# A decoder block on one core: the FFN input product without full blocks, with the first two block products of five pairs done ahead

## The chip, the cores and the metric

The kernel runs on one core of a Trainium2 chip. The metric is the time of one execution in microseconds (us) on the device. The engines are PE (TensorE, matrix products into PSUM banks of 128 x 512 float32), DVE (VectorE), ACT (ScalarE), POOL (GpSimd) and SP (SyncE, which issues nearly all transfers here). Each engine works through its own list of instructions in order and waits where one of them needs a result that isn't there yet.

## What is computed

One decoder block on 1024 tokens of width 1024: a dilated attention and a causal convolution module in parallel, merged by gates, projected and added to x; then a SwiGLU FFN with hidden width 2816. Everything is float32. The part that matters here is the end of the mix and the first half of the FFN:

```python
merged = jax.nn.sigmoid(z_ga) * y_attn + jax.nn.sigmoid(z_gc) * y_conv
x = x + rms_norm(merged @ w_mix_out[l], g_post_mix[l])
h = rms_norm(x, g_pre_ffn[l])
gate, up = jnp.split(h @ w_ffn_in, 2, axis=-1)
x = x + rms_norm((jax.nn.silu(gate) * up) @ w_ffn_out, g_post_ffn[l])
```

## The kernel before

**Products.** A float32 product is made of three fast ones: each operand is split into a high part (a cast, on ACT) and a low part (the difference, on DVE or POOL), and PE adds high x high, high x low and low x high. `split` does this for activations (lines 1286 and 1287), `part` (190, 191) and `both` (208, 209) for weights. `unit` multiplies one block of 128 output features by 512 tokens: 8 steps of three matmuls (lines 318 to 320). `prod` does the same over 4 steps (lines 334 to 336).

**Ticks.** After every step of three matmuls `tick` is called. It runs steps that `later` has put at that tick, then, at every `PIECE`-th tick, one piece of weight preparation from the queue `pieces`, then one step of each background generator in `gens`; a generator that yields n rests for n ticks. All of this only sets the order in which instructions are put on each engine's list.

**Weights.** The list `jobs` holds all weight blocks in order of use. `load_ahead` issues their transfers on SP up to a job, `queue_split` puts their pieces into the queue and moves the counter `queued` past them, `flush` runs what is left of a job's pieces. A pair of blocks ("row1", "row2") is a gate block and the up block that belongs to it, and is prepared by `quarters` in six steps: 0 splits A11 and A12, 1 makes the sums s12, 2 splits S1 and S2, 3 makes s34, 4 splits S3 and S4, 5 splits A22. `pair` is called ahead of each pair: it loads, queues and flushes what isn't done yet, and places steps 3 to 5 of this pair and 0 to 2 of the next at later ticks.

**The seven-product pair.** `winograd` computes a pair (2 x 2 blocks: gate and up by two halves of the tokens) with seven products in place of eight: A11 x B11, A12 x B21, S2 x T2, S1 x T1, S3 x T3, S4 x B22, A22 x T4. The B's are quarters of the activations h (two halves of the features by two halves of the tokens), T1 to T4 sums of them, made by `quarter_sums`. The products add up in the banks X, Z and V; f11, f22, f12 and f21 take the results out on DVE and ACT, and `sums` makes the operands of the last product of the FFN and stores them.

**The stretch in question.** The mix product goes over eight tiles of 128 tokens (line 1697). Behind each tile `mix_norm` runs in the background: two squares on ACT (1396), a row factor on DVE (`rstd_rows`, 1383 to 1388), gain and residual (1403, 1407), a store of the rows (1414), the second norm (1418, 1420). At tiles 3 and 7 the four tiles of a half are transposed on PE (1428), taken out with the gain on ACT (1434) and split. Then come the first `PLAIN` = 2 blocks of the FFN in full, as `ffn_half`: for each half of the tokens a gate unit with Silu and an up unit. The first halves of both run while tile 7 is normalised, the second halves while `quarter_sums` makes T1 to T4. The other 20 blocks are pairs through `winograd`.

## Time and profile before

| what | value |
|---|---|
| median of 3 runs | 1690.35 us (1689.8 to 1692.89) |
| the profiled execution | 1690.83 us, of which its span 1689.0 us |
| busy share of the span | PE 99%, DVE 75%, ACT 48%, POOL 30% |
| granted clock of PE | 0.999 |

The span runs from the first to the last instruction in the trace. "L334" is line 334 of the kernel, and a helper's line stands for all who call it. In the rows of groups the first number behind the bar is the busy time of the group in us, the second the mean ns of one; then comes the engine's idle time before them and who ended it. In the rows in order of time the first number is the start in us, the second the duration; an arrow in brackets says how long the engine had waited and for whom. In the rows of waits stand the sum, the number and the longest. "p" is a PSUM bank, "b" a buffer of 128 x 1024, "c" one of 128 x 512, "d" one of a ring of three.

### The profile page before, as it was taken

The page shows a single profiled execution, that of the slowest core. Times are in us where ns is not written, and L with a number is a line of the kernel's source. Part 1 is how long each engine was busy: PE and PEld are TensorE (multiplying, and loading weights), DVE is VectorE, ACT ScalarE, POOL GpSimd, SP SyncE. Part 2 cuts the span into 40 slices and gives each one's busy share as a digit, 9 for nine tenths or more (in the row PEclk, how much of TensorE's full clock was granted, in tenths as well). Part 3 has the DMA queues.
Part 4 walks back from the last instruction along what each step waited for, and adds up shares of the span by engine and source line. Part 5 has one row for each costly group of instructions (what it writes and reads, how often), then busy time and mean ns, then how long its engine had stood idle before and what let it go on. Part 6 is the DMA issues. An engine that isn't in the chain of part 4 may idle for free.

```text
span 1689.0 us, 23464 instructions
## 1 busy us (share of the span) xinstructions
PE 1676.4 (99%) x8167; PEld 1403.7 (83%) x8167; DVE 1259.8 (75%) x2209; ACT 818.9 (48%) x1599; POOL 513.4 (30%) x399
## 2 busy tenths in 40 slices
PE   9999999999999999999999999999999999999998
PEld 7788888888888889999888888888888888888886
DVE  6789988788999777778886855765655566677686
ACT  6344334344444588888713456533333333354453
POOL 0017777888886265765200300000000000000000
PEclk9999999999999999999999999999999999999999
DMA  4252433455566987888998523032233222494334
GB/s 168 104 187 88 150 125 131 137 195 178 183 174 162 282 269 224 241 232 250 300 294 313 200 88 118 26 131 94 94 114 111 94 94 102 170 376 125 111 121 156
DMA packets 162563, 283.36 MB, mean 168 GB/s; under 512 B 47249, under 2 KB 78988, under 8 KB 162444
## 3 DMA queue, kind: packets, MB, share of 16 engines
q1 hardware_dynamic: 161948, 281.42, 51.1%
q8 instruction: 64, 1.05, 0.3%
q14 instruction: 55, 0.45, 0.1%
q0 software_dynamic: 352, 0.18, 0.1%
q10 hardware_dynamic: 144, 0.26, 0.0%
HBM read 191.10 MB, written 95.42 MB: 170 GB/s over the span
## 4 chain that ended last, share of the span: by engine, by line
PE 93%; DMA 3%; DVE 1%; POOL 1%; issue 1%; ACT 1%; SPq 0%; DVEq 0%; ACTq 0%; POOLq 0%
PE p L334 15%; PE p L335 15%; PE p L336 15%; PE p L1968 12%; PE p L966 5%; PE p L1697 5%; PE p L318 5%; PE p L320 5%; PE p L319 5%; PE p L967 3%; PE p L1082 2%; PE p L1153 2%; PE p L578 2%; PE p L1120 2%; DMA b<-dact 1%
## 5 line engine op out<-in xcount | busy, mean ns | idle before, releaser
L334 PE MATMUL p<-b,b 128*128 128x512 f32 x1204 | 468.7, 389 | 0.5 <-ACT c L353 0.3
L335 PE MATMUL p<-b,b 128*128 128x512 f32 x1204 | 468.4, 389 | 0.0
L336 PE MATMUL p<-b,b 128*128 128x512 f32 x1204 | 468.4, 389 | 0.0
L334 PEld LDWEIGHTS p<-b,b 128*128 128x128 f32 x1204 | 226.0, 188 | 48.6 <-DVE c L862 1.0
L336 PEld LDWEIGHTS p<-b,b 128*128 128x128 f32 x1204 | 226.0, 188 | 46.9
L335 PEld LDWEIGHTS p<-b,b 128*128 128x128 f32 x1204 | 226.0, 188 | 46.8
L1968 PE MATMUL p<-b,b 128*128 128x512 f32 x924 | 209.6, 389 | 0.0
L1968 PEld LDWEIGHTS p<-b,b 128*128 128x128 f32 x924 | 173.4, 188 | 36.0
L708 DVE SCALAR_TENSOR_TENSOR p<-b,par,p 128x511 f32<-128x511 f32 (+14 forms) x232 | 163.6, 740 | 0.0
L318 PE MATMUL p<-b,b 128*128 128x512 f32 x368 | 147.0, 399 | 0.0
L966 PE MATMUL p<-b,b 128*128 128x512 f32 x384 | 144.1, 407 | 0.0
L320 PE MATMUL p<-b,b 128*128 128x512 f32 x368 | 143.5, 390 | 0.0
L319 PE MATMUL p<-b,b 128*128 128x512 f32 x368 | 143.5, 390 | 0.0
L208 ACT CAST b<-d 128x1024 fp32r<-128x1024 f32 x86 | 90.6, 1054 | 105.2 <-POOL d L229 55.1
L209 POOL TENSOR_TENSOR b<-d,b 128x1024 fp32r<-128x1024 f32 x44 | 107.0, 2431 | 79.6 <-ACT b L208 72.3
L209 DVE TENSOR_TENSOR b<-d,b 128x1024 fp32r<-128x1024 f32 x42 | 51.3, 1222 | 101.1 <-ACT b L208 101.1
L1287 DVE TENSOR_TENSOR b<-b,b 128x512 fp32r<-128x512 f32 x133 | 92.5, 700 | 22.2 <-ACT b L1286 20.2
L967 PE MATMUL p<-b,b 128*128 128x256 f32 x384 | 107.7, 281 | 0.0
L1286 ACT CAST b<-b 128x512 fp32r<-128x512 f32 x133 | 82.3, 621 | 48.9 <-PE p L1968 18.6
L1095 ACT ACTIVATE c<-c,stat 128x128 f32<-128x128 f32 (+1 forms) x192 | 85.4, 449 | 13.4 <-DVE stat L1085 12.2
L1697 PE MATMUL p<-b,b 128*128 128x512 f32 x384 | 89.4, 391 | 0.0
L208 ACT CAST b<-b 128x1024 fp32r<-128x1024 f32 x47 | 49.6, 1054 | 81.4 <-POOL b L236 37.3
(233 smaller groups left out, 2915.1 us busy)
## 6 DMA issues: line engine op xcount, KB each, us to landing
b<-w_in SPq DMA_DIRECT2D x30, 512.0 KB, 4.9
dk<-c SPq DMA_DIRECT2D x48, 256.0 KB, 4.5
dq<-c SPq DMA_DIRECT2D x48, 256.0 KB, 3.5
b<-dq SPq DMA_DIRECT2D x48, 256.0 KB, 4.6
b<-dk SPq DMA_DIRECT2D x48, 256.0 KB, 6.8
b<-w_fi SPq DMA_DIRECT2D x24, 512.0 KB, 5.3
d<-w_in SPq DMA_DIRECT2D x23, 512.0 KB, 4.0
dqS<-c SPq DMA_DIRECT2D x44, 256.0 KB, 2.2
```

The source lines that it names most:

```text
L209: self.wsplit.tensor_tensor(lo, x, f(hi), op=OP.subtract)
L318: nc.tensor.matmul(ps, hi[:, s], a, start=kt == 0, stop=False)
L319: nc.tensor.matmul(ps, hi[:, s], b, start=False, stop=False)
L320: nc.tensor.matmul(ps, lo[:, s], a, start=False, stop=kt == nk - 1)
L334: nc.tensor.matmul(ps, hi[:, s], a, start=first and kt == 0, stop=False, skip_group_check=True)
L335: nc.tensor.matmul(ps, hi[:, s], b, start=False, stop=False, skip_group_check=True)
L336: nc.tensor.matmul(ps, lo[:, s], a, start=False, stop=kt == 3, skip_group_check=True)
L708: nc.vector.scalar_tensor_tensor(A[i][:, j:], src[i][:, :H - j], w[i], A[i][:, j:], op0=OP.mult, op1=OP.add)
L966: nc.tensor.matmul(ps, a, w, start=kt == 0, stop=kt == KT - 1, skip_group_check=True)
L967: nc.tensor.matmul(ps[:, 256:], b, w[:, :256], start=False, stop=kt == KT - 1, skip_group_check=True)
L1697: nc.tensor.matmul(banks[tt][nh], st, wt[:, nh * H:(nh + 1) * H], start=bool(kt == 0 and a), stop=bool(kt == KT - 1 and b))
L1968: nc.tensor.matmul(acc[t], x, y, start=first and e == 0, stop=last and e == 2, skip_group_check=True)
```

## The change

There is no block in full any more; all 22 are pairs. For the first `HEAD` = 5 pairs the two products that need only the first half of the tokens (A11 x B11 and A12 x B21) are done right behind the mix product by `head`, with the A11 and A12 weights loaded and split as jobs of their own, and their banks X kept. Then `tail` does the other five products of each of these pairs. The gate and row blocks of these pairs are loaded again for the sums, and step 0 of `quarters` does nothing for them. The last four tiles of tokens are no longer transposed together behind tile 7: `last_tokens` transposes each tile by itself some ticks after its norm, takes it out half on ACT and half on DVE, and makes its part of the sums; behind tile 7 it splits T2, T1, T3, B22 and T4 in this order. `tail` calls `need`, which issues what of these splits hasn't been issued. PSUM is one set of eight banks in this stretch. `limit` keeps the head weights from being loaded before tile 7.

```diff
-PLAIN = 2
+HEAD = 5
...
+    limit = 1 << 30
+    headed = ()
+
     def load_ahead(self, i):
+        i = min(i, self.limit)
...
         if c == 0:
+            if i in self.headed:
+                return
             h, w = self.both(r1)
             o["A11"], o["A12"] = (h[:, l], w[:, l]), (h[:, r], w[:, r])
...
-        while self.queued < min(self.sent, i + 1):
+        while self.queued < min(self.sent, min(i, self.limit) + 1):
...
-        todo = [(1, lambda: self.quarters(i, 3)), (8, lambda: self.quarters(i, 4)), (10, lambda: self.quarters(i, 5))]
+        short = i in self.headed
+        a, b = (4, 8) if short else (8, 10)
+        todo = [(1, lambda: self.quarters(i, 3)), (a, lambda: self.quarters(i, 4)), (b, lambda: self.quarters(i, 5))]
         if n < len(J) and J[n][2] == "row1":
             todo += [(LD, lambda: self.load_ahead(n + 1))]
-            todo += [(k, lambda c=c: self.quarters(n + 1, c)) for c, k in enumerate(PC)]
+            pc = PC if not short else (10, 10, 14) if n + 1 in self.headed else (10, 12, 18)
+            todo += [(k, lambda c=c: self.quarters(n + 1, c)) for c, k in enumerate(pc)]
             if self.conv_sums:
                 todo.append((22, self.channel_sum))
             self.queued = n + 2
...
+    def head(self, w, T, f11):
+
+        nc = self.nc
+        hi, lo = w
+        X, x1 = self.bank(), self.half()
+        self.prod(X, (hi[:, :H], lo[:, :H]), T["B11"], True, False)
+        nc.scalar.copy(x1, X)
+        Z = self.bank()
+        self.prod(Z, (hi[:, H:], lo[:, H:]), T["B21"], True, True)
+        return X, f11(Z, x1)
...
+    def tail(self, W, T, X, need, f12, f21, f22):
+
+        nc = self.nc
+        x2, v1 = self.half(), self.half()
+        need("T2")
+        self.prod(X, W["S2"], T["T2"], False, False)
+        nc.scalar.copy(x2, X)
+        V = self.bank()
+        need("T1")
+        self.prod(V, W["S1"], T["T1"], True, False)
+        nc.scalar.copy(v1, V)
+        need("T3")
+        self.prod(X, W["S3"], T["T3"], False, False)
+        f22(X, v1)
+        v1 = None
+        need("B22")
+        self.prod(V, W["S4"], T["B22"], False, True)
+        rest = f12(V, x2)
+        V = x2 = None
+        need("T4")
+        self.prod(X, W["A22"], T["T4"], False, True)
+        rest()
...
+        if tt > 3:
+            yield from self.last_tokens(tt, hn)
+            return
...
+                y = self.feature(x, kt)
+                nc.scalar.activation(y, ps.rearrange("p (t n) -> p t n", t=4), AF.Copy, scale=self.col(C_PREF + kt))
...
+    def last_tokens(self, tt, hn):
+
+        nc = self.nc
+        o = (tt - 4) * 128
+        if tt == 4:
+            self.raw2 = [self.slot() for _ in range(4)]
+
+        def two(x):
+            return x[:, 2 * o:2 * o + 256]
+
+        add, stt = nc.vector.tensor_tensor, nc.vector.scalar_tensor_tensor
+        yield 6
+        for q in range(2):
+            ps = self.bank()
+            for i in range(4):
+                kt = 4 * q + i
+                nc.tensor.transpose(ps[:, i * 128:(i + 1) * 128], hn[:, kt * 128:(kt + 1) * 128], self.ident)
+            if q == 1:
+                hn = None
+            for i in range(4):
+                kt = 4 * q + i
+                d = two(self.raw2[kt // 2])[:, kt % 2 * 128:kt % 2 * 128 + 128]
+                if i % 2 == 0:
+                    nc.scalar.activation(d, ps[:, i * 128:(i + 1) * 128], AF.Copy, scale=self.col(C_PREF + kt))
+                else:
+                    nc.vector.tensor_scalar(d, ps[:, i * 128:(i + 1) * 128], self.col(C_PREF + kt), None, op0=OP.mult)
+            ps = None
+            yield 0
+        b11, b12, b21, b22 = self.raw1[:2], self.raw2[:2], self.raw1[2:], self.raw2[2:]
+        for i in range(2):
+            add(two(b11[i]), two(b11[i]), two(b12[i]), op=OP.subtract)
+        if tt > 5:
+            t2 = self.t2
+            for i in range(2):
+                stt(two(t2[i]), two(b11[i]), -1.0, two(b22[i]), op0=OP.mult, op1=OP.subtract)
+        if tt < 7:
+            yield 0
+            for i in range(2):
+                add(two(b12[i]), two(b22[i]), two(b12[i]), op=OP.subtract)
+            return
+        T = self.T
+        self.raw1 = self.raw2 = self.g_mix = self.t2 = None
+
+        def keep(name, x):
+            for k in range(4):
+                y = self.split(self.feature(x[k // 2], k), H)
+                T[name].append((y[:, :H], y[:, H:]))
+                if k % 2:
+                    x[k // 2] = None
+                yield (0, 1)[k % 2]
+
+        yield from keep("T2", list(t2))
+        yield from keep("T1", b11)
+        for i in range(2):
+            add(two(b12[i]), two(b22[i]), two(b12[i]), op=OP.subtract)
+        yield 0
+        yield from keep("T3", b12)
+        yield from keep("B22", b22)
+        for i in range(2):
+            stt(b21[i], t2[i], -1.0, b21[i], op0=OP.mult, op1=OP.subtract)
+            t2[i] = None
+            yield 1
+        yield from keep("T4", b21)
...
+    def early_sums(self):
+        b11, b22 = self.raw1[:2], self.raw2[2:]
+        self.t2 = [self.slot() for _ in range(2)]
+        for i in range(2):
+            a, b, c = (x[i][:, :512] for x in (self.t2, b11, b22))
+            self.nc.vector.scalar_tensor_tensor(a, b, -1.0, c, op0=OP.mult, op1=OP.subtract)
+            yield 1
...
+    heads = [job(aps["w_fi"][j]) for j in range(HEAD)]
+    fi = [pair2(j) for j in range(FT)]
+    B.headed = [fi[j] for j in range(HEAD)]
...
-            B.banks(g=6, s=2)
+            B.banks(g=8)
...
+        if tiles[0] == 7:
+            B.limit = 1 << 30
+            for n, j in enumerate(heads):
+                B.later(max(8 * n, 3), lambda j=j: B.load_ahead(j))
+                B.later(max(8 * n, 3) + 8, lambda j=j: B.queue_split(j))
+            B.later(16 + 8 * HEAD - 22, lambda: B.load_ahead(fi[0]))
+            for c, n in ((0, 12), (1, 12), (2, 6)):
+                B.later(16 + 8 * HEAD - n, lambda c=c: B.quarters(fi[0], c))
+            B.later(10, lambda: B.bg(B.early_sums()))
...
-    def ffn_half(j, hf, W):
-        o = B.half()
-        ps = B.unit(W[0], B.rhs(B.h2[hf]), KT)
-        nc.scalar.activation(o, ps, AF.Silu)
-        ps = B.unit(W[1], B.rhs(B.h2[hf]), KT)
-        nc.vector.tensor_tensor(o, ps, o, op=OP.mult)
-        held[j, hf] = o
...
-    for j in range(PLAIN):
-        Ws.append((B.weights(fi[j][0]), B.weights(fi[j][1])))
-        ffn_half(j, 0, Ws[j])
-    B.finish(norms[-1])
-    B.g_mix = None
-    h2 = [[(x[:, :H], x[:, H:]) for x in y] for y in B.h2]
-    qs = B.bg(B.quarter_sums(B.h2f, (h2[0][:4], h2[0][4:], h2[1][4:])))
-    h2 = None
-    for j in range(PLAIN):
-        ffn_half(j, 1, Ws[j])
-        Ws[j] = None
-    B.summed = lambda: None
-    B.first_sums(qs)
...
+    todo, silus = [], []
+    for j in range(HEAD):
+        f11, *rest = outs(j)
+        B.flush(heads[j])
+        X, r = B.head(B.hl.pop(heads[j]), B.T, f11)
+        silus.append(r)
+        if j >= 2:
+            while silus:
+                silus.pop(0)()
+        todo.append((X, rest))
+    X = rest = r = None
+
+    def need(name):
+        while len(B.T[name]) < 4:
+            next(norms[-1][0])
...
+    for j in range(FT):
+        w = B.pair(fi[j])
         if j == FT - 1:
             for k in range(LEAD):
                 loads(k)
             B.bg(first())
-        B.winograd(w, B.T, f11, f12, f21, f22)
+        if j < HEAD:
+            X, rest = todo[j]
+            todo[j] = None
+            B.tail(w, B.T, X, need, *rest)
+            X = rest = None
+        else:
+            B.finish(norms[-1])
+            B.winograd(w, B.T, *outs(j))
```

More of the change, by code (lines that the diff above doesn't have):

```diff
@@ L1646, in build @@
     if B.tags["g"] == 2:
-        B.banks(g=6, s=2)
+        B.banks(g=8)
     mop = [[None] * 8, [None] * 8]
@@ L1848, in first, with outs @@
             yield 3
-    for j in range(PLAIN, FT):
+    def outs(j):
         s = [None, None]
@@ L1883, in f21 @@
                 sums(p, held[0], None, held[1], None)
-        w = B.pair(fi[j][1])
+        return f11, f12, f21, f22
+    todo, silus = [], []
[14 more added lines that the diff above has]
+        w = B.pair(fi[j])
         if j == FT - 1:
```

50 lines of the change are left out of this document (22 added, 28 removed).

## The prediction

> **What bounds the kernel now.** I read the page first, then the waits of PE, then windows and rows of the stretch that is rewritten (by the last two rows of the fence: the mix product is done at 1043.9 us of the span, when ACT takes its last tile, and the chain is on `prod`, the first seven-product pair, by 1091.4).
>
> ```profile
> span 1689.0 us, 23464 instructions
> PE 1676.4 (99%) x8167; PEld 1403.7 (83%) x8167; DVE 1259.8 (75%) x2209; ACT 818.9 (48%) x1599; POOL 513.4 (30%) x399
> ...
> PE p L1082 <- DMA b<-dk: 1.3, 1, 1.3
> ...
> PE p L1082 <- DVE stat L1085: 0.2, 1, 0.2
> ...
> 1043.92 0.60 ACT L1396 ACTIVATE d<-p 128x512 f32<-128x512 f32 x1 [1.18 <-PE p L1697]
> ...
> 1091.39 0.23 PE p L334
> ```
>
> PE is busy for 99% of the span, and its list of waits has eight rows, of which the first and the last are shown: none is over 1.3 us. So each matmul removed is time removed, as long as the other engines go on delivering in time. Whether they do is asked of the stretch itself:
>
> ```profile
> core 0: us, DVE busy (x), PEclk, DMA share, GB/s
> 1043.90:1071.00 27.10, 16.10 (x32) 1.00 0.30 107
> 1071.00:1100.10 29.10, 25.75 (x41) 1.00 0.05 19
> 1100.10:1109.70 9.60, 8.27 (x13) 1.00 0.29 111
> ```
>
> DVE (VectorE) is 75% busy on the mean, but from 1071.0 to 1100.1 it works with hardly a pause: 41 instructions, 0.71 us each. That is the work of the sums and high/low splits T1 to T4, done while PE still has plain blocks to run. It fits there only because PE has 47 us of plain blocks ahead of the first pair. The change takes most of this cover away.
>
> **Matmuls removed.**
>
> ```profile
> 1022.32 21.79 PE p L1697 x96
> ...
> 1060.01 0.44 PE p L1428 x4
> ```
>
> In the chain of work 96 matmuls take 21.79 us: 0.227 us each, and a group of four transposes 0.44. A plain block has 4 units of 8 x 3 = 96 matmuls, a seven-product pair 7 x 4 x 3 = 84. Two blocks become pairs: 24 matmuls, 24 x 0.227 = **5.45 us less**. The transposes stay 64.
>
> **What stands before the first dependent product.** After the mix product PE now has five heads of two products (5 x 24 = 120 matmuls, 27.2 us) and four groups of transposes, two of tile 6 and two of tile 7 (1.8 us): 29.0 us. Then comes S2 x T2 of pair 0. Before, between the same point and the first dependent product stood 47 us of plain blocks and 24 matmuls (5.4 us) of the first pair.
>
> DVE's queue is in order, so I add up what is issued on it from the end of the mix product until the low half of S1|S2 of pair 0 is written. Prices:
>
> ```profile
> 1071.23 0.69 DVE L1287 TENSOR_TENSOR b<-b,b 128x512 fp32r<-128x512 f32 x1
> 1071.84 0.68 DVE L391 TENSOR_TENSOR c<-b,b 128x512 f32<-128x512 f32 x1
> 1072.56 0.69 DVE L392 SCALAR_TENSOR_TENSOR b<-c,b 128x512 f32<-128x512 f32 x1
> ...
> 1098.28 1.22 DVE L209 TENSOR_TENSOR b<-b,b 128x1024 fp32r<-128x1024 f32 x1
> 1099.41 0.69 DVE L1287 TENSOR_TENSOR b<-b,b 128x512 fp32r<-128x512 f32 x1
> ...
> L540 DVE TENSOR_TENSOR b<-b,b 128x256 fp32r<-128x256 f32 x12 | 4.5, 422 | 0.0
> L1085 DVE CUSTOM_DVE_ANT_0 c<-p,c 128x128 f32<-128x128 f32 x104 | 25.9, 287 | 4.2 <-PE p L1082 3.2
> ```
>
> From start to start a 512-wide operation takes 0.61 us (1071.23 to 1071.84), 0.72 if the next needs its result, a 1024-wide one 1.13 (0.08 to 0.09 under its duration). By the same difference a 256-wide one takes 0.34 and a 128-wide one from PSUM 0.21; the new 128-wide evictions have no row of their own, and the 287 ns row is the nearest.
>
> - rest of tile 6: 4 evictions, 6 sums of 256 (0.84 + 2.04): 2.9
> - norm of tile 7, by the rows below (1.5 + 1.3, and 12 small ones of 0.15 to 0.22): 4.7
> - low halves of the head weights 1 to 4, eight of 512: 4.9
> - five adds f11: 3.1
> - tile 7: 4 evictions, 4 sums of 256: 2.2
> - splits T2, T1, T3 and three of B22, fifteen of 512, and two sums of 256. The background step yields so that these are issued within the 40 ticks of the heads: 9.8
> - quarters 1 and 2 of pair 0, placed at ticks 44 and 50 counted from the start of tile 7: two sums and a split (0.72 + 0.61 + 1.13): 2.5
> - the same again: 2.5. `pair` calls `queue_split`, and the counter `queued` stands behind the last head, since the timed steps don't move it. So the three pieces of pair 0 are queued once more, and `flush` runs them ahead of its first product; step 0 does nothing for a headed pair, steps 1 and 2 are repeated, and W["S2"] is the second copy. They stand in DVE's queue behind f11 of the last head, which needs PE's last head product.
>
> Sum: 32.6 us of DVE work, to be set against 29.0 us and 0.45 for the two matmuls that need only the high half.
>
> ```profile
> 1044.64 0.15 DVE L1398 TENSOR_SCALAR ss<-ss 128x1 f32<-128x1 f32 x1 [1.09 <-ACT d L1396]
> 1045.22 0.16 DVE L1384 TENSOR_TENSOR rr<-ss 128x1 f32<-128x1 f32 x1 [0.42 <-ACT d L1396]
> 1045.55 0.17 DVE L1385 RECIPROCAL rr<-rr 128x1 f32<-128x1 f32 x1 [0.17 <-ACT rr L1383]
> 1051.25 0.16 DVE L1384 TENSOR_TENSOR rr<-ss,eps_rms 128x1 f32<-128x1 f32 x1 [1.05 <-ACT b L1418]
> ...
> L1403 DVE SCALAR_TENSOR_TENSOR d<-p,rr,b 128x512 f32<-128x512 f32 x2 | 1.5, 748 | 0.0
> L1407 DVE TENSOR_TENSOR d<-d,c 128x512 f32<-128x512 f32 x2 | 1.3, 684 | 0.0
> L1386 DVE SCALAR_TENSOR_TENSOR rr<-rr 128x1 f32<-128x1 f32 x2 | 0.4, 222 | 0.1
> ...
> 1046.57 1.28 ACT L1747 ACT_TABLE_LOAD   x1
> 1097.18 1.05 ACT L208 CAST b<-b 128x1024 fp32r<-128x1024 f32 x1
> ```
>
> DVE's own waits for ACT (ScalarE) come on top. Least: the norm's 1.09 + 0.42 + 0.17 + 1.05 + 0.17 = 2.9, and the cast of S1|S2 between its sum and its low half, 1.05 (L208): 4.0. Most: in 1043.9 to 1071.0 DVE idled 27.1 - 16.1 = 11.0 us around the same norm; two of the Silu table changes in it (1.28 each) go, as the first three Silus are held back past the norm: 8.4, with the cast 9.4. So the low half comes 36.6 to 42.0 us after the mix product and PE waits 36.6 - 29.45 = 7.2 to 12.5 us in this stretch, at the first tail product and before it in single waits for head weights that DVE and ACT deliver late. I take 11.5, nearer the upper end: the queues are in order, so a DVE that stands at a norm step takes nothing later in its place, and the Silus with one table load (1.28) stand in ACT's queue ahead of the T1 casts.
>
> **Smaller terms.**
>
> ```profile
> 1033.04 0.60 ACT L1396 ACTIVATE d<-p 128x512 f32<-128x512 f32 x1
> ...
> 1040.55 1.15 ACT L1420 ACTIVATE b<-d,rr 128x1024 f32<-128x1024 f32 x1 [0.87 <-DVE rr L1388]
> ...
> b<-w_fi SPq DMA_DIRECT2D x24, 512.0 KB, 5.3
> ```
>
> Transposes of tiles 5 and 6: a tile's normalised rows are ready 8.7 us after its first square (1033.04 to 1041.70). The squares now stand in ACT's queue behind evictions of the tile before, whose second transposes stand after the first six matmuls of the next tile: some 2.7 us later, so 11.4 and, with the four sums of 256 on DVE in between (0.34 each), up to 12.8. PE reaches the transposes after 48 matmuls and the transposes of the tile before, 10.9 + 0.9 = 11.8. Between 0 and 1.0 us each; 0.5 taken twice: **1.0**.
>
> Rest of tail 0: before its last product DVE has ten operations of 512 (the last split of B22, four of T4, two sums and A22 of the weights, f22, f12) and three of 1024, 6.1 + 3.4 = 9.5 us, against four products of 12 x 0.227, 10.9 us: 0, or up to 1.8 where f22 and the S3|S4 split stand behind these; taken as **0.8**. From tail 1 on DVE has some 9 to 10 us to do in 13.6 us of PE, and it costs nothing.
>
> Five more weight loads, 512 KB each, land 5.3 us after issue. Those of heads 3 and 4 are queued on SP behind the store of tile 7's rows, which is written some 8 us after the mix product, and they are needed at some 18 and 23 us: covered, 0; without this cover a load costs its 5.3. The low half of head 0 that POOL still does ends before the mix product or within head 0's first product: 0. PSUM as one set of eight banks: at most five kept, two of a transposing tile and one running; 0, or, where a running bank is given out again at once, the time that f11 is behind, up to 2 us.
>
> Sum: -5.45 + 11.5 + 1.0 + 0.8 = **+7.85 us**. The profiled execution took 1690.83 us for a span of 1689.0 and stands 0.48 above the median 1690.35 of the runs; the same change of 7.85 on that median gives **1698.2**. With the ends of the terms: 7.2 - 5.45 = +1.8 and 12.5 + 2.0 + 1.8 + 2 - 5.45 = +12.9, so 1692 to 1703.
>
> **Rivals.**
> 1. *The cover holds* (0.08, faster): DVE's idle time closes up and the sums of tiles 4 to 6, now done inside the mix product, are enough to get S1|S2 and T2 out in 29.4 us. Then 1690.35 - 5.45 = 1684.9. It decides at the low half of S1|S2 of pair 0: with 4.0 us of forced idle, 7.2 of my 32.6 us would have to be missing. For it: the sums of tiles 4 and 5, eight of 256, and two of 512 are issued before the mix product ends. Against it: these are left out of my list already.
> 2. *The repeated quarters don't cost* (0.13, about no change): were the queue counter moved past pair 0, or the first copy used, 2.5 us of sums and splits and a cast of 1.05 would go from the end of the chain: stall 3.7 to 9, and the time 1688.6 to 1696, likeliest 1691. Against it: nothing in the diff moves the counter.
> 3. *The clock falls after the long wait* (0.10, slower still): the granted clock is 1.00 in the three windows above, where PE never waited over 1.3 us, so nothing shows what a wait of 4 to 9 us does to it. Were it halved for the next 10 to 20 matmuls, each would cost 0.227 more: 2.3 to 4.5 us, 1700.5 to 1702.7. [...] No run here shows it yet.
> 4. *Banks* (0.05): PE held at each head by a bank that f11 has not read, beyond what the sum has, up to 2 us at four heads: 1703 to 1709.
>
> **How the numbers follow.** The forecast (slower through DVE's queue) has 0.64. About 0.2%, 3.4 us, is what a measurement of this kernel can tell from no change: 1687 to 1693.7. Faster: all of rival 1 and 0.04 of rival 2, 0.12. Same: 0.05 of rival 2 and 0.05 of the forecast's low end, 0.10. Slower: 0.78. The range 1690 to 1703 takes in the forecast, rival 3 and most of rival 2; it leaves out rivals 1 and 4 and a part of rival 2, under 2 in 10.
>
> **What would show it.** PE's waits should have new rows at the first product of `tail`, on the S1|S2 casts and splits of `both`, 4 to 9 us at once, and short ones on `part`'s splits in `head` and on the normalised rows in `last_tokens`. The windows should show DVE without pause from some 10 us after the mix product until the middle of tail 1, and two runs of quarters 1 and 2 for pair 0. Matmul records of a product should add up to 24 fewer. From the mix product to the end of the fifth pair, 192 + 3 x 84 matmuls and eight groups of transposes or 104 us before, it should be some 111 us. I am wrong if PE shows no wait over 2 us there (rival 1), or if the wait is there but the second run of the quarters isn't (rival 2).

## The result, and the profile after

The changed kernel takes 1709.28 us (median of 5 runs, 1707.31 to 1713.3) against 1690.35: a ratio of 1.0114, 95% interval 1.0097 to 1.013. It is slower by 18.9 us where 7.85 were forecast. The profiled execution took 1708.97 us for a span of 1707.2, 18.2 more than before.

In the rows below L343 to L345 are the three matmuls of `prod`, L1839 the mix product, L1512 the transposes of `last_tokens` with their evictions L1519 (ACT) and L1521 (DVE), L1471 the normalised rows, L194 and L195 the cast and the low half of `part`, L212 and L213 those of `both`, L234 and L235 the sums s12, L241 and L242 the sums s34, L1333 and L1334 the split of `split`, L402 the copy of x2, L1565 the early sums of T2, L1960 the add of f11, L1962 the Silu.

The page's head and PE's list of waits (sum, number, longest):

```profile
span 1707.2 us, 23474 instructions
PE 1681.2 (98%) x8143; PEld 1402.4 (82%) x8143; DVE 1276.8 (75%) x2251; ACT 818.6 (48%) x1613; POOL 512.7 (30%) x399
```

```profile
PE p L343 <- ACT b L212: 4.9, 1, 4.9
PE p L343 <- ACT b L194: 3.0, 3, 1.4
PE p L345 <- DVE b L195: 2.6, 3, 1.5
PE p L1512 <- ACT b L1471: 2.2, 2, 1.9
```

There are 24 matmuls fewer, as forecast, and the four rows of waits that the forecast named: 4.9 us at the first product of `tail`, 5.6 in the heads, 2.2 at the transposes, 12.7 in all (13.3 with the 0.8 for the rest of the tail were in its sum). The waits of PE came as forecast. The windows show what did not:

```profile
core 0: us, PE busy (x) PEld busy (x) DVE busy (x) ACT busy (x) POOL busy (x), PEclk, DMA share, GB/s
1034.00:1043.90 9.90, 8.31 (x34) 6.83 (x35) 4.45 (x17) 4.07 (x10) 0.00 (x0) 0.83 0.16 57
...
1049.00:1059.00 10.00, 7.56 (x36) 5.55 (x34) 7.72 (x20) 5.71 (x15) 1.30 (x1) 1.00 0.26 83
...
1072.00:1082.00 10.00, 7.17 (x27) 5.07 (x28) 7.86 (x13) 8.28 (x15) 0.00 (x0) 0.95 0.00 0
1082.00:1090.00 8.00, 7.78 (x22) 5.73 (x21) 5.96 (x11) 5.93 (x11) 0.00 (x0) 0.64 0.07 14
...
1095.00:1110.00 15.00, 14.96 (x60) 11.76 (x60) 13.51 (x18) 6.64 (x11) 0.00 (x0) 0.90 0.00 1
```

From 1082 to 1090 PE is busy for 7.78 of 8 us and gets through 22 matmuls, 0.36 us each in place of 0.227; the granted clock is 0.64. PE's rows in order of time:

```profile
1057.54 0.50 PE L343 MATMUL p<-b,b 128*128 128x512 f32 x1 [1.43 <-ACT b L194]
1057.87 0.40 PE L344 MATMUL p<-b,b 128*128 128x512 f32 x1
1059.25 0.50 PE L345 MATMUL p<-b,b 128*128 128x512 f32 x1 [0.98 <-DVE b L195]
1059.58 0.39 PE L343 MATMUL p<-b,b 128*128 128x512 f32 x1
...
1079.36 0.50 PE L343 MATMUL p<-b,b 128*128 128x512 f32 x1 [0.92 <-ACT b L194]
...
1081.58 0.80 PE L345 MATMUL p<-b,b 128*128 128x512 f32 x1 [1.49 <-DVE b L195]
1082.17 0.63 PE L343 MATMUL p<-b,b 128*128 128x512 f32 x1
1082.60 0.63 PE L344 MATMUL p<-b,b 128*128 128x512 f32 x1
...
1087.72 0.44 PE L344 MATMUL p<-b,b 128*128 128x512 f32 x1
```

From 1082.17 to 1087.72 stand 13 steps of 0.43 us: half speed, behind two waits of 0.92 and 1.49 us. Behind 1.43 and 0.98 us at 1057 to 1059, the same 2.41 in sum, the clock stayed up: the step that follows takes 0.33 us (1059.25 to 1059.58), the next 0.23. From the windows, one less the clock times the length: 1.7 us lost at the transposes, 0.5 + 2.9 late in the heads, 1.5 behind the wait of 4.9, 6.6 in all.

The second of the forecast's signs, quarters 1 and 2 of pair 0 done twice, is in DVE's rows:

```profile
1079.51 0.68 DVE L234 TENSOR_TENSOR d<-b 128x512 f32<-128x512 f32 x1
1080.23 0.69 DVE L235 TENSOR_TENSOR d<-d,d 128x512 f32<-128x512 f32 x1
...
1087.33 1.23 DVE L213 TENSOR_TENSOR b<-d,b 128x1024 fp32r<-128x1024 f32 x1 [1.63 <-ACT b L212]
1088.47 3.09 DVE L1334 TENSOR_TENSOR b<-b,b 128x512 fp32r<-128x512 f32 x5
1091.48 0.68 DVE L1960 TENSOR_TENSOR c<-p,c 128x512 f32<-128x512 f32 x1
1092.08 0.68 DVE L234 TENSOR_TENSOR d<-b 128x512 f32<-128x512 f32 x1
1092.80 0.69 DVE L235 TENSOR_TENSOR d<-d,d 128x512 f32<-128x512 f32 x1
1094.65 1.22 DVE L213 TENSOR_TENSOR b<-d,b 128x1024 fp32r<-128x1024 f32 x1 [1.17 <-ACT b L212]
```

The first S1|S2 was complete when L213 ended at 1088.56. PE's next product started at 1094.67, since it uses the second copy, whose sums stand behind the last f11 (1091.48). That f11 did not wait for PE, whose last head matmul had started at 1089.39: it stood in DVE's queue behind five splits of the T's and B22 (L1334, 3.09 us).

**By stages**, with the times of both traces. The fifth pair ends 17.2 us later (1165.7 for 1148.5: the first L362 of the sixth pair, 1173.90, less three products of 2.72 us). That is the same 17.2 by which the last matmul of this FFN product starts later (1489.0 for 1471.8); what comes behind adds 1.0.

| term | forecast | measured | from |
|---|---|---|---|
| 24 matmuls | -5.45 | -5.45 | x8143 for x8167 |
| mix product, tiles 5 and 6 | +1.0 | +3.3 | its end 1049.0; 1043.9 + 1.8 of transposes = 1045.7 |
| mix product to first tail product | +11.5 | +16.6 | 1049.0 to 1094.67 = 45.7, less 29.0 (the 0.45 of the first two tail matmuls is in the next row) |
| tails | +0.8 | +2.9 | 1094.67 to 1165.7 = 71.0, less 300 x 0.227 |
| sum | +7.85 | +17.35 | |

In the middle term PE's waits are 10.8 (4.9, 5.6 and 0.3 at the transposes of tile 6). The other 5.8 are, counted on PE's own rows, 3.4 of half clock and some 2 for starting again: behind a wait the first step takes 0.33 us, 0.10 more, and from the step before it 0.15 more pass than the named wait (1059.25 - 1057.87 = 1.38 = 0.227 + 0.98 + 0.17), 0.25 at each of eight waits.

### The profile page after: what moved, and what is told of

Read it like the earlier page. It is cut to its first block, busy times and chain, and to the rows that moved or that the text cites. A ratio compares the mean times of both kernels' runs of the same rounds, so it can differ in the third digit from the quotient of the medians.

```text
span 1707.2 us, 23474 instructions
## 1 busy us (share of the span) xinstructions
PE 1681.2 (98%) x8143; PEld 1402.4 (82%) x8143; DVE 1276.8 (75%) x2251; ACT 818.6 (48%) x1613; POOL 512.7 (30%) x399
## 3 DMA queue, kind: packets, MB, share of 16 engines
q8 instruction: 64, 1.05, 0.3%
## 4 chain that ended last, share of the span: by engine, by line
PE 46%; DVE 3%; ACT 2%; DMA 1%; issue 1%; DVEq 0%; SPq 0%; ACTq 0%
PE p L2099 12%; PE p L345 8%; PE p L343 8%; PE p L344 8%; PE p L1839 4%; PE p L327 2%; PE p L328 2%; PE p L329 2%; DMA b<-dw 1%; ACT b L1333 0%; DVE b L1334 0%; DMA b<-dact 0%; ACT b L1469 0%; ACT b L194 0%; DVE d L1458 0%
## 5 line engine op out<-in xcount | busy, mean ns | idle before, releaser
L343 PE MATMUL p<-b,b 128*128 128x512 f32 x1260 | 493.3, 392 | 8.4 <-ACT b L212 4.9
L345 PE MATMUL p<-b,b 128*128 128x512 f32 x1260 | 492.8, 391 | 2.7 <-DVE b L195 2.6
L343 PEld LDWEIGHTS p<-b,b 128*128 128x128 f32 x1260 | 237.6, 189 | 61.2 <-ACT b L212 5.3
L345 PEld LDWEIGHTS p<-b,b 128*128 128x128 f32 x1260 | 237.5, 188 | 55.2 <-DVE b L195 4.4
L344 PEld LDWEIGHTS p<-b,b 128*128 128x128 f32 x1260 | 237.7, 189 | 49.0
L2099 PEld LDWEIGHTS p<-b,b 128*128 128x128 f32 x924 | 173.4, 188 | 37.2 <-DVE c L1982 1.2
L212 ACT CAST b<-d 128x1024 fp32r<-128x1024 f32 x86 | 90.4, 1051 | 111.1 <-POOL d L235 55.1
L213 POOL TENSOR_TENSOR b<-d,b 128x1024 fp32r<-128x1024 f32 x44 | 106.9, 2430 | 79.8 <-ACT b L212 72.3
L213 DVE TENSOR_TENSOR b<-d,b 128x1024 fp32r<-128x1024 f32 x42 | 51.3, 1221 | 93.2 <-ACT b L212 93.2
L1334 DVE TENSOR_TENSOR b<-b,b 128x512 fp32r<-128x512 f32 x133 | 91.5, 695 | 17.5 <-ACT b L1333 15.8
L1333 ACT CAST b<-b 128x512 fp32r<-128x512 f32 x133 | 81.6, 619 | 45.3 <-PE p L2099 20.4
L212 ACT CAST b<-b 128x1024 fp32r<-128x1024 f32 x49 | 51.6, 1052 | 99.5 <-POOL b L242 37.2
L1839 PE MATMUL p<-b,b 128*128 128x512 f32 x384 | 91.5, 396 | 0.0
```

The lines of the kernel that those rows point to most:

```text
L212: self.nc.scalar.copy(hi, x)
L213: self.wsplit.tensor_tensor(lo, x, f(hi), op=OP.subtract)
L343: nc.tensor.matmul(ps, hi[:, s], a, start=first and kt == 0, stop=False, skip_group_check=True)
L344: nc.tensor.matmul(ps, hi[:, s], b, start=False, stop=False, skip_group_check=True)
L345: nc.tensor.matmul(ps, lo[:, s], a, start=False, stop=kt == 3, skip_group_check=True)
L1839: nc.tensor.matmul(banks[tt][nh], st, wt[:, nh * H:(nh + 1) * H], start=bool(kt == 0 and a), stop=bool(kt == KT - 1 and b))
```

## The experiments

Three theories stood. **A, the cover**: DVE has more to do than PE's plain work covers. **B, the order**: the work would fit, but stands in the wrong place in in-order queues (the repeated quarters behind f11, single waits that each cost). **C, the clock**: short waits bring half clock, and PE loses more than it waits. Each kernel was timed beside the kernel before (1691.19, 1690.24, 1690.78 and 1690.58 us in the four sets of runs); "over" is against that. An interval reaches some 2.5 us to either side, so a difference of under 3 us between two kernels is a hint and not more.

### e1_once: the quarters of pair 0 once

```diff
+    B.queued = fi[0] + 1
     for j in range(FT):
         w = B.pair(fi[j])
```

> The counter of queued jobs is moved past pair 0 before the tails, so quarters 1 and 2 of pair 0 run once; nothing else is changed. Median of the changed kernel 1709.3 us, of the kernel before 1690.35. Theory A (DVE's whole queue is too long for the cover): the 2.5 us of DVE work that go shorten the 4.9 us wait at the first tail product by about that, and a wait for the T3 or B22 splits takes over some of it; 1706 to 1707. Theory B (the order: the second run stands behind f11 of the last head): the first copy of S1|S2 is written at 1088.6 us of the changed kernel's span, before PE ends its heads at 1089.6, so the whole wait of 4.9 us goes, and with it the half clock behind it (1.5 us): 1702 to 1703.

1705.15 us, ratio 1.0078 [1.0063, 1.0093], 4.1 under the changed kernel. Of the wait of 4.9 us 0.2 is left, and small ones have come in tail 0, 3.0 us in all:

```profile
PE p L345 <- DVE b L213: 1.1, 2, 0.6
PE p L343 <- ACT c L402: 1.1, 1, 1.1
```

The repeat costs about what rival 2 gave it (2.5 + 1.05), yet taking it away does not bring the time near 1691: between A and B.

### e2_warm: PE kept running

```diff
+    def warm(n):
+        d = B.bank()
+        for i in range(n):
+            nc.tensor.matmul(d, B.T["B11"][0][0][:, :128], B.T["B11"][0][0], start=i == 0, stop=i == n - 1)
...
         B.flush(heads[j])
+        if j:
+            warm(8)
...
+            if j == 0:
+                warm(20)
```

52 matmuls whose result nobody reads, at the places where PE waited.

> Adds matmuls that nothing reads, on operands that are long there: 8 at the start of each of heads 1 to 4 (1.8 us each) and 20 before the first tail product (4.5 us), together 52 matmuls or 11.8 us of PE work. Theory C (the clock is halved because PE stood idle): PE's granted clock stays at 1.00 behind the mix product, the steps of 0.43 us between matmuls go, and as the added work lies where PE waited the time falls by 1 to 4 us from 1709.3, to 1705 to 1708. If the clock falls for another reason, the added work only moves the waits and costs what doesn't fit into them: 1709 to 1715, with steps of 0.43 us still there.

1708.78 us, ratio 1.0103 [1.0088, 1.0118].

```profile
1049.00:1072.00 23.00, 21.28 (x100) 17.00 (x100) 16.81 (x43) 12.30 (x28) 1.28 (x1) 1.00 0.44 157
1072.00:1082.00 10.00, 10.00 (x46) 8.29 (x45) 7.86 (x13) 9.04 (x16) 0.00 (x0) 1.00 0.00 0
1082.00:1095.00 13.00, 10.52 (x47) 8.38 (x45) 10.18 (x17) 7.59 (x13) 0.00 (x0) 1.00 0.23 83
```

11.8 us of added matmuls (52 x 0.227) cost nothing, and from the heads on the clock stays at 1.00 up to the wait of 2.9 us that is left (behind it, at 1097.26, it falls to 0.50): the clock falls because PE pauses. But the time is the same: at the first tail product PE still stands for what ACT and DVE deliver, and half clock in the heads was not what made that late.

### e3_evict and e4_nolow: a bank for each engine; less work on DVE

```diff
-                if i % 2 == 0:
+                if q == 0:
                     nc.scalar.activation(d, ps[:, i * 128:(i + 1) * 128], ...
```

> Each bank of transposes of the last four tiles is taken out by one engine (the first bank by ACT, the second by DVE) instead of by both in turn. In the changed kernel each ACT eviction waits some 0.4 us for the DVE one before it on the same bank. Theory B: a pair of banks is out 1 to 1.5 us earlier, the norm behind it starts earlier, the waits of the transposes for the normalised rows (1.87 and 0.29 us) shrink to under 1 us together and the half clock behind them goes: 2 to 4 us less, 1705 to 1707. Theory A: the DVE work is the same, so the first tail product and the heads start as late as before: 1708 to 1710.

1706.21 us, ratio 1.0094 [1.0071, 1.0116], 3.1 under the changed kernel. There the two engines took turns on one bank, as its rows of ACT and DVE show:

```profile
1053.77 0.37 ACT L1519 ACTIVATE b<-p,par 128x128 f32<-128x128 f32 x1 [0.42 <-DVE b L1521]
...
1053.12 0.61 DVE L1521 TENSOR_SCALAR b<-p,par 128x128 f32<-128x128 f32 x2 [0.44 <-ACT b L1519]
```

Each eviction waits for the other engine's. With a bank each, the last matmul of the heads starts at 1083.5 in place of 1089.4, but the first tail product only 4.5 us earlier (1090.16): its wait grows from 4.9 to 6.2.

e4 leaves the low halves of T1 to T4 and B22 out and uses the high half in their place: about 12.2 us less for DVE, 9.2 of them (15 of 20 splits) ahead of the first tail product.

```diff
-                y = self.split(self.feature(x[k // 2], k), H)
-                T[name].append((y[:, :H], y[:, H:]))
+                y = self.slot(F32R)
+                nc.scalar.copy(y[:, :H]..., self.feature(x[k // 2], k))
+                T[name].append((y[:, :H], y[:, :H]))
```

> Leaves out the low halves of T1 to T4 and B22 (the products use the high half in their place): 20 DVE operations of 512, 12.2 us, are gone, 15 of them before the first tail product; PE does the same matmuls. Theory A: without 9.2 us of DVE work ahead of it the first tail product waits 0 to 1 us and the heads less; 1699 to 1702. Theory B: the second run of quarters still stands behind f11 of the last head and takes 0.4 + 0.7 + 1.3 + 1.05 us, so 3 to 3.5 us of the 4.9 stay, and so do the waits in heads 1 to 3: 1705 to 1707.

1704.67 us, ratio 1.0072 [1.0056, 1.0089]. 12.2 us of DVE work less buy 4.6 us, and the two largest waits stay:

```profile
PE p L343 <- ACT b L212: 3.9, 1, 3.9
PE p L343 <- ACT b L194: 3.1, 3, 1.4
```

By the forecast's sum (32.6 - 9.2 = 23.4 us of DVE work and 4.0 to 9.4 of its waits for ACT, 27.4 to 32.8 against 29.45) 0 to 3.4 us should have been left before and at the first tail product, where 7.0 are left in these two rows alone. DVE does less and waits longer for ACT's casts: 14.4 us from the mix product to its low half of S1|S2, 10.7 in the changed kernel. So less work on DVE alone does not end these waits. Against A as forecast, for B.

### f1, f2, f3, f4: order mended, POOL helping, earlier weights, six heads

f1 is e1 and e3 together. f2 adds POOL for the low halves of the head weights, f3 to that earlier loads of the heads, f4 is f2 with six heads.

```diff
# f2, in part
-        (nc.vector if c == 0 else self.wsplit).tensor_tensor(lo[:, s], ...
+        (nc.gpsimd if i in self.pooled else nc.vector if c == 0 else self.wsplit).tensor_tensor(lo[:, s], ...
# f3, behind tile 7
+            B.PIECE = 2
-                B.later(max(8 * n, 3), lambda j=j: B.load_ahead(j))
-                B.later(max(8 * n, 3) + 8, lambda j=j: B.queue_split(j))
+                B.later((3, 5, 6, 16, 24)[n], lambda j=j: B.load_ahead(j))
+                B.later((9, 12, 16, 24, 32)[n], lambda j=j: B.queue_split(j))
# f4
-HEAD = 5
+HEAD = 6
```

> The two edits together: quarters 1 and 2 of pair 0 once (4.1 us less by itself) and each bank of transposes taken out by one engine (3.1 us less by itself), against 1709.3 of the changed kernel. If the two act at different places the sum stands: 1702. If the wait at the first tail product only moves to the next products (theory A), 1703 to 1705.

> As the run before, and the low halves of the head weights are made by POOL, which has nothing to do in this stretch, in place of DVE: 4.9 us of DVE work less, each low half 0.6 us later by POOL's longer duration. Theory B (order: these splits stand in DVE's queue among the steps of the norm): the waits at the third matmul of the heads (2.6 us in the changed kernel) fall to under 1 us, and the half clock behind them goes: 3 to 4 us under the run before, 1698 to 1699. Theory A: the same, and the waits in the first tail go as well: 1696 to 1697. If POOL's accesses slow DVE down, no gain.

> As the run before, and the weights of heads 0 to 2 are loaded at ticks 3, 5 and 6 of tile 7, ahead of the store of tile 6's rows in SP's queue, and all head weights are split 4 to 8 ticks earlier. Theory B: the casts of heads 1 to 4 no longer stand in ACT's queue behind steps of the norm that wait, so the waits at the first matmul of the heads (3.0 us in the changed kernel) go: 2 to 4 us under the run before. If ACT's total work is the limit there, the norm is later by as much and nothing is won.

> As the POOL run, with six heads in place of five: 5.45 us more cover ahead of the first tail product, and no matmul more or less. Theory A (cover): the waits of the first tail (3.3 us in the run with the quarters once) go, 2 to 4 us under the POOL run. Theory B: the waits inside the heads stay, one more head adds up to 1 us of them: within 2 us of the POOL run.

| kernel | us | ratio [95%] | over |
|---|---|---|---|
| f1_once_evict | 1699.57 | 1.0054 [1.0037, 1.007] | 9.3 |
| f2_pool | 1701.3 | 1.0061 [1.0044, 1.0079] | 11.1 |
| f3_early | 1701.4 | 1.006 [1.0043, 1.0077] | 11.2 |
| f4_six | 1703.91 | 1.0075 [1.006, 1.009] | 13.7 |

f1 is 9.7 under the changed kernel, more than its parts (4.1 + 3.1): once the repeat is gone, an earlier end of the heads is no longer given back at the first tail product. Two edits of place that leave all of A's needed work in are worth half of the 18.9. POOL in f2 wins nothing:

```profile
PE p L346 <- POOL b L196: 2.5, 5, 0.7
```

PE now waits five times for POOL where it had waited twice, 2.5 us in all, for DVE (the low halves are L196 here). And the 4.9 us of work taken off DVE come back as longer operations beside POOL's. Six operations on two SBUF operands that DVE starts while POOL works end only when POOL has ended, 0.3 to 1.1 us longer than elsewhere in this trace, 4.9 us in all; f11 and the evictions, which read PSUM, keep their time. One of the six (elsewhere 0.68 us):

```profile
1074.92 1.29 POOL L196 TENSOR_TENSOR b<-b,b 128x512 fp32r<-128x512 f32 x1 [3.50 <-issue]
1074.99 1.77 DVE L235 TENSOR_TENSOR d<-b 128x512 f32<-128x512 f32 x1
```

In f3 the waits on head weights are gone, and PE stands at the transposes:

```profile
PE p L1513 <- ACT b L1472: 5.5, 3, 3.3
```

It reaches them sooner than tile 7's rows. f4 with its sixth head is 2.6 us over f2, no more than a hint, with waits for POOL of 3.0 in all and 1.6 for the cast of S1|S2.

### g1, g2: the Silus too, and all together

g1 is f1 with the Silus of the five headed pairs issued in `tail`, so that neither they nor the table load stand in ACT's queue ahead of the casts. g2 is f3 with that and with the transposes 8, 6 and 10 ticks behind the norms (tiles 4 and 5, 6, 7) in place of 6.

```diff
-            while silus:
-                silus.pop(0)()
...
-    def tail(self, W, T, X, need, f12, f21, f22):
+    def tail(self, W, T, X, need, f12, f21, f22, silu):
...
+        silu()
         need("T3")
...
# g2
-        yield 6
+        yield 8 if tt < 6 else 6 if tt == 6 else 10
```

> As f1_once_evict (1699.6 us), and the Silus of the first five pairs are issued in their tails, not behind heads 2 to 4: a table load and five Silus, 3.9 us of ACT work, leave the heads. Theory B (what stands ahead in ACT's queue): the waits at head 4 (0.93 us on ACT's cast, 1.49 on DVE's low half behind it) fall to under 1 us together and the T1 casts come earlier: 1697 to 1698.5. If DVE alone sets these, no change: 1699 to 1700.

> The edits of f3_early and g1_late_silu together, and the transposes of a tile stand later in PE's list (8 ticks behind the norm for tiles 4 and 5, 10 for tile 7, 6 before), so that PE should not stand at them. In f3_early the waits inside the heads were gone, but PE stood 5.5 us at the transposes. If the waits come from positions alone they now go together: 1693 to 1696. If the chain of tile 7 (norm, transposes, sums, T2) is as long as the heads, the wait comes back at the first tail product: 1698 to 1701.

g1: 1697.87 us, ratio 1.0042 [1.0027, 1.0058]. g2: 1695.79 us, ratio 1.0025 [1.0014, 1.0037], the best of all, and still over the kernel before. What is left of the waits, and DVE's and ACT's rows around the longest:

```profile
PE p L344 <- ACT c L403: 2.9, 2, 2.6
PE p L1514 <- ACT b L1473: 2.3, 3, 1.0
```

```profile
1084.89 0.69 DVE L243 TENSOR_TENSOR b<-d,d 128x512 f32<-128x512 f32 x1
...
1085.66 1.04 ACT L213 CAST b<-b 128x1024 fp32r<-128x1024 f32 x1 [1.66 <-DVE b L243]
...
1087.13 0.58 ACT L403 COPY c<-p 128x512 f32<-128x512 f32 x1
```

```profile
1073.00:1098.00 25.00, 22.21 (x90) 17.31 (x88) 24.28 (x36) 15.76 (x26) 0.23 (x1) 0.93 0.00 1
```

The copy of x2 (L403), for which PE waits, stands in ACT's queue behind the cast of S3|S4 (L213), and that stood 1.66 us for DVE's sums s34 (L243). DVE is busy for 24.28 of 25 us there: in this window, with the order mended, its work is the bound, which is A. Earlier it is not. On g2's chain of work that ended last, four groups of DVE operations (at 1051.6, 1053.9, 1057.4 and 1067.9 us) take 2.23, 1.76, 1.29 and 1.90 us beside POOL's low halves, where the same forms without POOL take 0.67, 0.67, 0.17 and 0.67 in this trace: 5.0 us of the chain, about what POOL took over (4.9). The same order without POOL was not run.

### g4, g5: fewer heads; the last tiles transposed together

```diff
# g4, on top of g1
-HEAD = 5
+HEAD = 4
# g5, on the changed kernel: last_tokens keeps the rows of tiles 4 to 7
+        self.late = getattr(self, "late", []) + [hn]
+        if tt < 7:
+            return
         yield 6
-        for q in range(2):
+        for q in range(8):
+            hn, o, q = self.late[q // 2], q // 2 * 128, q % 2
...
-            B.later(10, lambda: B.bg(B.early_sums()))
```

> As g1_late_silu with four heads in place of five: 5.45 us less cover ahead of the first tail product, the same number of matmuls. Theory A and the chain as the limit: 4 to 6 us over g1_late_silu. If each head brings its own waits (six heads took 2.6 us more than five): within 1.5 us of g1_late_silu.

> One part of the change undone: the last four tiles are transposed together behind the norm of tile 7, as before, and their sums made in one piece; heads, tails and the repeated quarters are as in the changed kernel (1709.3 us). Behind the mix product stand then eight groups of transposes and evictions (four times two) and four more 1024-wide sums of 1.13 us each. If tile by tile is what makes the chain short: 6 to 9 us over the changed kernel, 1715 to 1718. If the waits that tile by tile brings into the mix product (2.2 us and the half clock behind them) outweigh that: 1706 to 1709.

g4: 1702.8 us, ratio 1.0072 [1.0055, 1.0089], 4.9 over g1. Five heads give 27.2 us of matmuls as cover, four 21.8, and the waits move to the splits of the sums:

```profile
PE p L343 <- ACT b L1334: 2.4, 1, 2.4
...
PE p L344 <- DVE b L1335: 2.3, 1, 2.3
```

Nearly all of the 5.4 us of cover taken away is lost. This is A again, shown from the other side, in a kernel whose order is mended and in which POOL does not make these low halves.

g5: 1705.81 us, ratio 1.0093 [1.0073, 1.0113], 3.5 under the changed kernel where 6 to 9 over it were expected. The expectation missed. The mix has no wait and its clock stays at 1.00, and the waits are two:

```profile
PE p L343 <- ACT b L194: 6.0, 1, 6.0
PE p L343 <- ACT b L212: 5.9, 1, 5.9
```

Two long waits cost no more than the many short ones of the changed kernel: transposing tile by tile, for which the evictions stand in turns and PE stops in the mix, wins nothing as it is ordered here. Whether it loses the 3.5 us is less sure: the intervals of the two kernels overlap.

### h1, h2, h3: what g2 lacks

h1 gives the sums and low halves S1 to S4 of pair 0 to POOL, ahead of the first tail; h2 puts 12 matmuls that nobody reads ahead of S3 x T3 of tail 0; h3 is h1 with the transposes of tiles 5 and 6 later, those of tile 6 inside the first head.

```diff
# h1, on top of g2, in quarters
+        old = self.wsplit
+        if self.headed and i == self.headed[0] and c < 5:
+            self.wsplit = nc.gpsimd
...
-            for c, n in ((0, 12), (1, 12), (2, 6)):
+            for c, n in ((0, 12), (1, 12), (2, 9), (3, 5), (4, 3)):
# h2, on top of g2, in tail
+        if first:
+            d = self.bank()
+            for i in range(12):
+                nc.tensor.matmul(d, T["B11"][0][0][:, :128], T["B11"][0][0], start=i == 0, stop=i == 11)
         silu()
# h3, on top of h1
-        yield 8 if tt < 6 else 6 if tt == 6 else 10
+        yield 8 if tt == 4 else 9 if tt == 5 else 8 if tt == 6 else 10
...
-    for e in norms[:-1]:
-        B.finish(e)
```

> As g2_all (1695.8 us), and the sums and low halves of S1 to S4 of pair 0 are made by POOL in place of DVE (7.1 us of DVE work less), steps 3 and 4 ahead of the first tail product. In g2_all DVE ran without pause from 1073 to 1098 us and PE stood 2.6 us at S3 x T3, for a copy that ACT had queued behind the S3|S4 cast. Theory A (DVE's total is what is left): that wait and the half clock behind it (2 us) go, 1691 to 1693. If POOL's longer times (2.43 us for a 1024-wide operation) make S1|S2 late instead: 1695 to 1698.

> As g2_all, with 12 matmuls that nothing reads (2.7 us) where PE stood 2.6 us, ahead of S3 x T3 of the first tail. If standing still is what halves the clock there: the steps of 0.43 us behind it go, and the time is that of g2_all less 1.5 to 2 us, 1694. If not: the same time with the steps still there, 1696.

> As h1_pair0_pool, and the transposes of tiles 5 and 6 stand 3 and 2 steps later in PE's list, those of tile 6 inside the first head in place of right behind the mix product. PE stood 0.8 and 1.0 us at them in g2_all. If that is position alone: 1.5 to 2 us less than h1_pair0_pool, 1690 to 1691.5. If the sums of tile 6 now delay the norm of tile 7 in DVE's queue by as much: no change.

h1: 1699.35 us, ratio 1.0053 [1.0036, 1.0069], 3.6 over g2. h3: 1698.97 us, ratio 1.005 [1.0035, 1.0065], no difference from h1. The relief for DVE is none: while POOL works on pair 0, DVE's splits of the T's take up to 2.43 us in place of 0.68. So the sum for T3 is late, ACT stands 5.21 us for it (3.50 in g2), and PE waits longer for the copy of x2 (L409 here), which is queued behind the casts that follow:

```profile
PE p L350 <- ACT c L409: 4.1, 1, 4.1
```

h2: 1696.13 us, ratio 1.0034 [1.0021, 1.0047]. No difference from g2 that the runs can tell.

```profile
1082.00:1095.00 13.00, 12.27 (x54) 9.62 (x52) 12.74 (x19) 10.05 (x17) 0.00 (x0) 1.00 0.01 2
```

```profile
PE p L345 <- DVE c L1977: 1.8, 1, 1.8
```

The clock that was 0.87 in this window of g2 is 1.00, and PE waits 1.8 us for DVE a little later. The full clock by itself bought nothing here.

## Why the prediction was right or wrong

**Right: the direction, the places of the waits and, partly by luck, their size.** There are 24 matmuls fewer; new waits stand at the rows named, 12.7 us for 13.3; the quarters run twice, which was worth 4.1 us in e1 where the forecast priced it at 2.5 + 1.05. Rival 1 (the cover holds) is out: PE waits 4.9 us at the first tail product, no version without waits was found, and g4 shows cover to be short by about what is taken from it. Rival 4 (banks): none of PE's waits names the copy or the f11 that free a bank at the heads. The size of the waits is partly luck. A wait is the time at which DVE and ACT deliver less the time at which PE gets there, and both came out some 6 us later than forecast: 46.9 us for 40.95 (below), and 36.1 (46.9 less 10.8 of waits) for 29.45.

**Wrong: the time, by 11 us.** The step that failed is the sum of DVE's queue in "What stands before the first dependent product". It has the low half of S1|S2 ready 36.6 to 42.0 us after the mix product, 40.95 as taken (29.45 + 11.5). It started at 1094.65 and ended at 1095.87, 46.9 us after 1049.0. In that stretch DVE is busy for 35.7 us, not 32.6, and idle for 11.2, not 4.0 to 9.4. Of the work, one early sum took 1.81 us in place of 0.68 beside POOL; the forecast had left it out as done before the end of the mix product. The idle time (sum, number, longest):

```profile
DVE b L195 <- ACT b L194: 3.2, 3, 1.7
DVE b L213 <- ACT b L212: 2.8, 2, 1.6
DVE b L1334 <- ACT b L1333: 2.7, 3, 2.0
DVE b L1521 <- ACT b L1519: 1.7, 4, 0.4
DVE rr L1436 <- ACT rr L1434: 0.3, 2, 0.2
```

The forecast took these waits from the rows of the norm, which cost 0.3 us here, and one cast of 1.05. They lie at the casts of the head weights, of S1|S2 and of the T's, and at the evictions: 10.4 us. ACT in turn waits 17.5 us for DVE in this stretch. Neither engine's list of waits names PE there, and the chain of work that ended last has no piece of PE between 1039.3 and 1094.67 us: it goes back and forth between DVE and ACT. That exchange sets the time of the first tail product.

**The clock, rival 3.** Counted on PE's rows, the excess over the forecast in the three stretches of the table (2.3, 5.1 and 2.1 us) looks like what PE lost beside its waits: half clock 1.7, 3.4 and 1.5, and some 2 us of starting again in the heads. Rival 3 stood outside the sum, with 2.3 to 4.5 us behind one long wait; the runs showed half clock behind short waits as well. In the heads, though, PE is not on the chain: e2 kept the clock at 1.00 there and won 0.5 us, which is nothing that the runs can tell. In the mix and behind the first tail product PE is on the chain, so there half clock counts. What it costs by itself, with nothing else late, no run here isolates.

In the changed kernel no long wait was needed: 13 steps at half speed followed waits of 0.92 and 1.49 us. In its trace the granted clock goes to 0.50 at 1036.60, 1080.98 and 1094.63 us and back to 1.00 at 1040.03, 1087.81 and 1098.05, whole multiples of some 3.41 us apart, as on a grid. PE was busy for 1.60 us of the cell of this grid from 1077.57 to 1080.98, and the clock was 0.50 in the next; it was busy for 1.98 us of the cell from 1057.09 to 1060.50, and the clock stayed at 1.00. In e1 the half clock lasts 3.41 us, eight steps of 0.43 from 1058.89 on. Counted from there in cells of that length, nearly the same four waits fall otherwise, and it is the reverse: 1.76 us busy from 1055.48 to 1058.89 and then 0.50, 2.11 and 2.32 us in the two cells from 1075.96 and 1.00 behind each. What sets the clock is not shown beyond these cells.

**Order, and not only the amount of DVE's work.** The forecast let 32.6 us of DVE's work decide. e4 took 9.2 us of it away and 3.9 of the 4.9 us wait stayed; e1 and e3 changed only places and the repeat and won 9.7 together. Order is what the runs could win back: the repeat behind f11 (4.1), evictions in turns on one bank (3.1, priced at nothing in the forecast), Silus and their table load ahead of casts (1.7 from f1 to g1, a hint). The forecast did argue that "the queues are in order" but turned it into a choice of 11.5 between 7.2 and 12.5, not into rows of its own. Behind these the amount of work is a bound (DVE 24.28 of 25 us in g2; the head less in g4). What the 5.0 us are made of by which g2 still stands over the kernel before, on top of the 5.45 that the 24 matmuls save, is not shown in full: what DVE's operations take longer beside POOL's is 5.0 us of its chain, but the low halves would have taken DVE about as long.

**Mis-sized: the transposes of tiles 5 and 6**, 0.5 us each as taken, 3.3 in the mix product of the trace (a wait of 1.9 and half clock behind it, 0.83 over 9.9 us) and a wait of 0.3 behind it. In g5, without them, PE is busy for the whole of the mix.

**Open.** The 1.0 us behind the FFN's first product, and why a head with less cover costs nearly all of what it covered (g4) while one more (f4) costs too: f4 is built on f2, where the head weights were still late, so it does not bound the best number of heads in g2's order.

## What to carry to other kernels

Before plain work is taken away from in front of dependent work, write down each in-order queue as rows with what each waits for; a cast or sum queued behind an operation that comes late is late too, however idle its engine is. Two engines that wait for each other in turn make a chain that is longer than the work of either (46.9 us here, with DVE busy for 35.7), so follow the chain that ended last before you blame the engine that stands still. Count a wait of PE for more than its length where PE is on that chain (some 0.25 us more here, and steps of 0.43 us in place of 0.227 where the clock halved). Where two engines empty one bank, give each a bank of its own (3.1 us in e3). Move work from DVE to POOL only if its longer operations (1.29 us in f2, 0.68 on DVE) are not awaited one by one and DVE has no work on two SBUF operands meanwhile (1.77 us in place of 0.68 there).

## What the runs showed of the hardware that was not expected

- The granted clock halved behind short waits in the changed kernel: 13 steps of 0.43 us in place of 0.227 behind waits of 0.92 and 1.49 us, none behind 1.43 and 0.98. It changed some 3.41 us, or whole multiples of that, apart; of the cells of this length at full clock that were given above, those with 1.60 (changed kernel) and 1.76 us (e1) of busy PE were followed by 0.50, those with 1.98 (changed kernel), 2.11 and 2.32 (e1) by 1.00. With matmuls put into the waits (e2 in the heads, h2 in the first tail) it stayed at 1.00.
- DVE's operations on two SBUF operands took longer beside POOL's: 1.81 us in place of 0.68 for an early sum in the changed kernel, 1.77 in place of 0.68 in f2, 1.29 in place of 0.17 for a 128x1 operation in g2. In f2 operations from PSUM did not: f11 took 0.68 or 0.69 us there too.
- A wait of PE cost some 0.25 us beyond its named length at full clock: in the changed kernel 0.17 around the wait of 0.98 us before 1059.25, and 0.10 in the step behind it, 0.33 us in place of 0.227.
- ACT's and DVE's evictions of the same PSUM bank did not overlap: 0.42 to 0.44 us of wait at each change of engine. Each eviction at such a change waits for the other engine's, and with a bank each (e3) the kernel was 3.1 us faster.
